# A one-core hybrid decoder step: the GLA and mLSTM branches rewritten as generators that run one step after each weight granule

## The chip, the cores and the metric

The kernel runs on one core of one Trainium2 chip. The core has a matrix engine (PE in the profile, with its weight loads as PEld), a vector engine (DVE), an activation engine (ACT), GpSimd (POOL) and a sequencer that only issues transfers (SP); POOL and ACT can issue transfers too. Each engine takes its instructions in a fixed order. The metric is the device time of one execution in microseconds, the median of the runs shown.

## What is computed

One layer of a recurrent decoder for 256 prompt rows and 8 × 4 sample rows, 288 columns in all, everything in fp32. The heads of the reference are these:

```python
proj = xn @ P['w_in']
(lru_x, g_q, g_k, g_v, g_lr, g_gate, m_x, m_o, m_if, mg) = jnp.split(proj, _split_points(), axis=-1)
...
o, gla_S_new = gla_chunked(q, k, v, logdec.reshape(B, T, GLA_HEADS, GLA_DK), gla_S)
y_gla = rmsnorm(o.astype(dt), P['gla_g_norm']).reshape(B, T, GLA_HEADS * GLA_DV) * jax.nn.silu(g_gate)
...
mq = blockdiag(mc, P['ml_w_q']).reshape(B, T, MLSTM_HEADS, MLSTM_DH)
mk = blockdiag(mc, P['ml_w_k']).reshape(B, T, MLSTM_HEADS, MLSTM_DH) * (MLSTM_DH ** -0.5)
...
h, C_new, n_new, m_new = mlstm_chunked(mq, mk, mv, gates[..., :MLSTM_HEADS], gates[..., MLSTM_HEADS:], ml_C, ml_n, ml_m)
y_ml = jax.nn.sigmoid(m_o) * rmsnorm(h.astype(dt), P['ml_g_norm']).reshape(B, T, MLSTM_WIDTH)
...
merged = (gate[:, :, 0] * (y_lru @ P['w_br_lru'])
          + gate[:, :, 1] * (y_gla @ P['w_br_gla'])
          + gate[:, :, 2] * (y_ml @ P['w_br_ml']))
```

Then come `merged @ w_out`, the residual, a second norm and a squared-ReLU MLP (2048 to 8192 and back) with its residual, and a last norm. Shift, scale and gate of both norms come from `silu(c) @ w_ada`. GLA keeps a state of 128 × 256 for each of 4 heads, mLSTM one of 256 × 257 (memory and normaliser) for each of 4 heads, and the 8 sample sequences bring their own states in and out.

## The kernel before, in words

**The projections.** All weights go through `stream` (lines 148 to 170). A *granule* is a weight tile of 128 × 1024 numbers, 512 KB. SP loads it into one of three `raw` buffers (line 155), ACT rounds it to `hi` (line 156), DVE takes the rest into `lo` (line 157), and PE does 24 matmuls of 288 columns with it (lines 163 to 165): `hi` by the upper and the lower half of the activations, `lo` by the upper half. There are 530 granules and 12,720 such matmuls; this document calls them the main matmuls.

**Work beside them.** `run` (line 184) walks a stream granule by granule. After each it does what `every` lists: `L` loads a tile of `w_ada` (the conditioning weights), `V` multiplies the tiles that are held (line 256). It also takes one step of each generator in `side`; the instructions of such a step are put on every engine behind the granule's last `hi`, `lo` and matmul. `slots` names the buffers that the `w_ada` tiles go to: `None` is a ring of one, a number is one of the ten activation slots, `"st"` the two tiles that also carry the recurrent states.

**The order.** A scheduler that replays a model of the engines sorts the instructions of each engine by readiness and priority. SP's transfers stay in the order of the program. PE, DVE, ACT and POOL wait in order too once the program is built: an instruction whose operand is late holds all behind it.

**The three branches.** The stages are: query, key and value projections; LRU input; gates; `merge(0)` (LRU); `B_MX`; `merge(1)` (GLA); `B_MO`; `merge(2)` (mLSTM); the output projection; the MLP. Each `merge` runs four times a gate block (8 granules) and a branch block (4 granules). LRU is a generator already (line 533). `gla` (line 689) is a plain function that is called once, in `merge(0)`, and `mlstm` (line 900) one that is called after the `B_MX` blocks; all their instructions stand at one place of the program, and the scheduler spreads them as it sees fit.

**GLA.** Cumulative decays, transposed keys and values, the scores, then per head four chunks in sequence through one state buffer `st` (line 770), and a loop over 8 state tiles of the samples: load (line 815), read-out on PE (line 818), update on PE and DVE (lines 825, 826), store (line 827). `spread` (line 679) makes the masked values for it on POOL, 128 × 2048 numbers for each head.

**mLSTM.** A causal convolution (line 530 on DVE), block-diagonal weights (line 915 on POOL), gate rows (lines 930 to 983), values and keys by time (lines 995, 1000), values and keys of the samples (1010, 1017), keys by feature `kf` (line 1022) and queries by feature `qf` (line 1029), then per head the weights `w0`, `w1` (lines 1038 to 1042), scores (1046, 1049), products (1056 to 1062) and the prompt's state (1069). Then a loop over 16 state tiles of the samples: load (line 1109), read-out (1113, 1116), update (1121, 1122), store (1123). All state transfers are issued by POOL, and the state tiles have two buffers (tag `st`). At the end the 8 squares are summed over rows (line 641), the root is inverted on 288 columns (lines 644 to 648) and the outputs are scaled (line 1146).

**The norms.** `rstd_of` (lines 383 to 388) takes the inverse root as Ln and Exp of 128 equal rows of 288.

Of the kernel before, what the change touches and what calls it, by code (L numbers as in the profile page):

```python
# [8 lines left out]
F32 = mybir.dt.float32  # L9
F32R = mybir.dt.float32r  # L10
AF = mybir.ActivationFunctionType
ALU = mybir.AluOpType
# [21 lines left out]
          ("wq", 32), ("wk", 32), ("wv", 32)]  # L34
# [18 lines left out]
def trunk(ctx, tc, io):  # L53
# [328 lines left out]

    def rstd_of(ps):
        r = row("lf")
        with tc.high_priority():
            S.activation(r, ps[:, :N], AF.Ln, bias=eps, scale=1.0 / D)
            S.activation(r, r, AF.Exp, scale=-0.5)
        return r
# [247 lines left out]
    def rows_rsqrt(src, add):  # L636

        p = longp()
        for e in range(2):
            for h in range(4):  # L640
                T.matmul(p[32 * h:32 * h + 32, :N], ones[:, 0:32], src[:, 2 * h + e, :], start=e == 0, stop=e == 1)
        r = row("rr")
        if add is None:
            S.activation(r, p[:, :N], AF.Sqrt, bias=eps, scale=1.0 / 256)
        else:
            V.scalar_tensor_tensor(r, p[:, :N], 1.0 / 256, add, ALU.mult, ALU.add)
            S.activation(r, r, AF.Sqrt)
        V.reciprocal(r, r)
        return r

    def by_sequence(qm, q):

        G.memset(qm, 0.0)
        G.tensor_copy(qm.rearrange("p n (b j) -> p n b j", b=NB)[:, :, :, 0:TS], smp(q))
# [13 lines left out]
    def parts(dst, src, sel, los):  # L668

        w = src.shape[-1]  # L670
        p = misc()
        T.matmul(p[:, 0:w], sel, src, start=True, stop=True)
        S.copy(dst, p[:, 0:w])
        for a, b in los:
            V.tensor_tensor(out=dst[a:b], in0=p[a:b, 0:w], in1=dst[a:b].bitcast(F32), op=ALU.subtract)

    def spread(vx, v, w):

        G.tensor_tensor(out=vx, in0=v.bitcast(F32).unsqueeze(1).to_broadcast([P, NB, w]),
                        in1=C("bcol").unsqueeze(2).to_broadcast([P, NB, w]), op=ALU.mult)  # L680
# [8 lines left out]
    def gla():  # L689
        g_cs, ee, kk_ = slot(4), slot(5), slot(3)  # L690
        wg2 = flat(kk_)[:, 4 * N:4 * N + 512]
        G.memset(wg2, 0.0)
        G.dma_start(wg2[0:32], io["wg2"])
        bg = Pm("bg")
        for h in range(4):
            p = misc()
            T.matmul(p[:, :N], wg2[:, h * P:(h + 1) * P], sm, start=True, stop=True)
            softlog(g_cs[:, h, :], p[:, :N], bg[:, h:h + 1], ee[:, h, :])
        S.activation(ee[:, 0:4], ee[:, 0:4], AF.Exp, scale=-1.0)
        S.activation(ee[:, 0:4], ee[:, 0:4], AF.Ln, bias=1.0)  # L700
        G.tensor_tensor(out=g_cs[:, 0:4], in0=g_cs[:, 0:4], in1=ee[:, 0:4], op=ALU.subtract)
        rm = resets(row("gc"), 0.0, 1.0, 64)
        for h in range(4):
            V.tensor_tensor_scan(g_cs[:, 4 + h, :], rm, g_cs[:, h, :], 0.0, ALU.mult, ALU.add)
        cs = g_cs[:, 4:8, :]
        TAU = 1.0 / 16
        S.activation(ee[:, 0:4], cs, AF.Exp, scale=TAU)
        S.activation(ee[:, 4:8], cs, AF.Exp, scale=-TAU)
# [3 lines left out]
        d_ = g_cs[:, 0:4, :]  # L712
        csp, dp = (a[:, :, 0:NP].rearrange("p h (c l) -> p h c l", c=4) for a in (cs, d_))
        V.tensor_tensor(out=dp, in0=csp[:, :, :, 63:64].to_broadcast([P, 4, 4, 64]), in1=csp, op=ALU.subtract)
        css, ds_ = smp(cs), smp(d_)
        G.tensor_tensor(out=ds_, in0=css[:, :, :, 3:4].to_broadcast([P, 4, NB, TS]), in1=css, op=ALU.subtract)
        S.activation(d_, d_, AF.Exp, scale=TAU)
        qe, ke = qk[:, 0:4, :], qk[:, 4:8, :]
        V.scalar_tensor_tensor(qe, qe, 128 ** -0.5, ee[:, 0:4], ALU.mult, ALU.mult)
        kd = kk_[:, 0:4, :]  # L720
        G.tensor_tensor(out=kd, in0=ke, in1=d_, op=ALU.mult)
# [4 lines left out]
        for t in range(2):  # L726
            for q in range(2):
                p = misc()
                for i in range(4):
                    T.transpose(p[:, i * P:(i + 1) * P], vv[:, 4 * q + i, t * P:(t + 1) * P], ident)  # L730
                S.copy(vt[:, t, 512 * q:512 * q + 512], p)
        vs = sc([P, 257], "vs", 1)
# [9 lines left out]
        S.copy(ks, p[:, 0:P])  # L742

# [5 lines left out]
        for c in range(2):  # L749
            for t in range(2):  # L750
                if c:
                    V.tensor_scalar(kdt[c][:, t, :], pk[t], C("half")[:, c:c + 1], None, ALU.mult)
                else:
                    S.activation(kdt[c][:, t, :], pk[t], AF.Copy, scale=C("half")[:, c:c + 1])

        bb = flat(slot(9))
        am = bb[:, 0:1024].rearrange("p (t h i) -> p t h i", t=2, h=4)
        st = bb[:, 1024:2048].rearrange("p (h e) -> p h e", h=4)
        for t in range(2):
# [5 lines left out]
            V.scalar_tensor_tensor(am[:, t], C("glo").unsqueeze(1).to_broadcast(bc), -1.0, am[:, t], ALU.mult, ALU.min)  # L765
        oT = slot(5)
        for h in range(4):
            po = longp()
            for e in range(2):
                for t in range(2):  # L770
                    c0 = e * 256 + t * P
                    T.matmul(po[:, c0:c0 + P], vt[:, t, h * 256 + e * P:h * 256 + (e + 1) * P], am[:, t, h, :],
                             start=e == 0 and t == 0, stop=False, skip_group_check=True)
            for c in range(4):
                if c:
# [637 lines left out]
```

## Time and profile before

| | |
|---|---|
| median of 3 runs (lowest, highest) | 2022.71 us (2020.01, 2024.82) |
| the profiled execution, its time | 2018.23 us |
| its span on the core | 2016.5 us |
| mean granted PE clock | 0.99 |
| PE busy | 1962.6 us, 97% |
| DVE, ACT, POOL busy | 1027.0, 805.7, 289.3 us |

A row of the groups of instructions reads: line, engine, operation, output and inputs, sizes, count, then busy time and mean duration, then the engine's idle time ahead of it and what ended it. A row of the timeline reads: start, duration, engine, line, operation. One of the stretches has, for each engine, busy time and count, then PE's clock as a share of full speed. A matmul of fp32 operands leaves two records, a main matmul one.

### The profile page before, as it was taken

How to read it: one execution, taken by the hardware profiler on the slowest of the kernel's cores; microseconds unless marked ns; L12 is line 12 of the kernel's file. 1: busy time of each engine (PE TensorE's matmuls, PEld its weight loads, DVE VectorE, ACT ScalarE, POOL GpSimd, SP SyncE). 2: the span in 40 equal slices, each digit the busy share in tenths (PEclk: the TensorE clock that was granted, in tenths of full speed). 3: DMA queues.
4: the chain of work that ended last, by engine and by line, in shares of the span. 5: the costliest groups of instructions: out<-in, count | busy, mean ns of one | idle time of the engine just before them, and what ended most of it. 6: DMA issues, size and time to landing. Idle time of an engine off the chain costs nothing.

```text
span 2016.5 us, 35281 instructions
## 1 busy us (share of the span) xinstructions
PE 1962.6 (97%) x14838; PEld 1838.8 (91%) x14838; DVE 1027.0 (51%) x1436; ACT 805.7 (40%) x1107; POOL 289.3 (14%) x339
## 2 busy tenths in 40 slices
PE   6999999999999999899999999999999999999997
PEld 4889888999997998799999989999999999999997
DVE  3463647646692466543444564335444444444564
ACT  3333464533364332333333454443343434343434
POOL 0300200212231223100011441000010101010101
PEclk8999999999999999899999999999999999999998
DMA  9988756546642377676779736654444454455443
GB/s 372 397 325 308 269 199 237 205 168 240 211 153 73 124 259 253 209 258 250 263 257 356 272 123 224 230 197 159 174 160 157 163 182 158 159 173 171 157 159 119
DMA packets 119438, 429.48 MB, mean 213 GB/s; under 512 B 11744, under 2 KB 11904, under 8 KB 119152
## 3 DMA queue, kind: packets, MB, share of 16 engines
q1 hardware_dynamic: 109776, 392.56, 54.9%
q0 software_dynamic: 7920, 28.92, 4.0%
q10 hardware_dynamic: 1584, 5.75, 0.8%
q8 instruction: 116, 1.90, 0.4%
q14 instruction: 42, 0.34, 0.1%
HBM read 410.38 MB, written 16.81 MB: 212 GB/s over the span
## 4 chain that ended last, share of the span: by engine, by line
PE 87%; DMA 5%; DVE 4%; issue 2%; ACT 1%; POOL 0%; SPq 0%; DVEq 0%; ACTq 0%; POOLq 0%
PE mm L163 26%; PE mm L165 26%; PE mm L164 25%; PE pa L256 4%; DMA raw<-win 3%; DVE lo L157 1%; DMA st<-mC 1%; DVE s L530 1%; DMA s<-wada 1%; ACT hi L156 1%; DMA o_C_s<-st 0%; PE px L579 0%; PE px L1069 0%; PE pi L1113 0%; PE px L781 0%
## 5 line engine op out<-in xcount | busy, mean ns | idle before, releaser
L157 DVE TENSOR_TENSOR lo<-raw,hi 128x1024 fp32r<-128x1024 f32 x450 | 583.7, 1299 | 626.9 <-ACT hi L156 612.0
L156 ACT ACTIVATE hi<-raw 128x1024 fp32r<-128x1024 f32 x450 | 476.4, 1060 | 831.4 <-PE mm L164 618.2
L163 PE MATMUL mm<-xh,hi 128*128 128x288 f32 x2576 | 761.6, 299 | 11.8 <-ACT hi L156 4.7
L164 PE MATMUL mm<-xl,hi 128*128 128x288 f32 x2576 | 759.3, 297 | 0.1
L165 PE MATMUL mm<-xh,lo 128*128 128x288 f32 x2576 | 739.3, 297 | 4.4 <-DVE lo L157 4.4
L163 PEld LDWEIGHTS mm<-xh,hi 128*128 128x128 f32 x2576 | 484.6, 189 | 36.5 <-issue 17.8
L163 PE MATMUL mm<-s,hi 128*128 128x288 f32 x1664 | 489.4, 297 | 0.0
L164 PEld LDWEIGHTS mm<-xl,hi 128*128 128x128 f32 x2576 | 486.2, 189 | 3.4 <-issue 2.1
L164 PE MATMUL mm<-s,hi 128*128 128x288 f32 x1664 | 489.0, 296 | 0.0
L165 PEld LDWEIGHTS mm<-xh,lo 128*128 128x128 f32 x2576 | 478.7, 189 | 8.6 <-DVE lo L157 5.9
L165 PE MATMUL mm<-s,lo 128*128 128x288 f32 x1664 | 476.4, 295 | 0.4 <-DVE lo L157 0.4
L163 PEld LDWEIGHTS mm<-s,hi 128*128 128x128 f32 x1664 | 311.8, 188 | 6.1 <-issue 5.4
L164 PEld LDWEIGHTS mm<-s,hi 128*128 128x128 f32 x1664 | 312.5, 188 | 0.3
L165 PEld LDWEIGHTS mm<-s,lo 128*128 128x128 f32 x1664 | 308.2, 188 | 2.7 <-issue 1.7
L157 DVE TENSOR_TENSOR lo<-s,hi 128x1024 fp32r<-128x1024 f32 x80 | 98.0, 1225 | 115.3 <-ACT hi L156 115.3
L1251 POOL TENSOR_TENSOR t<-t 128x288 f32<-128x288 f32 x64 | 60.5, 954 | 647.6 <-ACT t L1250 647.6
L156 ACT ACTIVATE hi<-s 128x1024 fp32r<-128x1024 f32 x80 | 84.9, 1061 | 143.3 <-PE mm L164 140.0
L881 POOL TENSOR_TENSOR s<-s,t 128x288 f32<-128x288 f32 x32 | 32.2, 1030 | 207.3 <-DVE t L880 207.3
L1267 DVE TENSOR_TENSOR s<-s,mm 128x288 f32<-128x288 f32 x96 | 40.3, 451 | 33.9 <-PE mm L165 32.6
L256 PE MATMUL pa<-s,silc 128*32 128x512 f32 (+1 forms) x480 | 51.7, 526 | 5.5 <-DMA s<-wada 5.5
L425 DVE TENSOR_TENSOR s<-t,s 128x288 fp32r<-128x288 f32 x64 | 33.9, 568 | 16.6 <-ACT s L424 16.6
L1122 DVE SCALAR_TENSOR_TENSOR st<-st,csb,px 128x257 f32<-128x257 f32 x64 | 28.5, 479 | 23.6 <-PE px L1121 15.9
(358 smaller groups left out, 1144.7 us busy)
## 6 DMA issues: line engine op xcount, KB each, us to landing
raw<-win SPq DMA_DIRECT2D x192, 512.0 KB, 4.7
raw<-wf SPq DMA_DIRECT2D x176, 512.0 KB, 4.2
s<-wada SPq DMA_DIRECT2D x47, 1024.0 KB, 8.9
s<-wf SPq DMA_DIRECT2D x80, 512.0 KB, 3.5
ag<-wada SPq DMA_DIRECT2D x29, 1024.0 KB, 6.0
raw<-wout SPq DMA_DIRECT2D x32, 512.0 KB, 6.0
st<-wada SPq DMA_DIRECT2D x28, 512.0 KB, 6.8
s<-win SPq DMA_DIRECT2D x14, 768.0 KB, 6.8
```

What stands on the lines that cost most here:

```text
L156: pace["hi"] = S.activation(hi, raw, AF.Copy)
L157: pace["lo"] = V.tensor_tensor(out=lo, in0=raw, in1=hi.bitcast(F32), op=ALU.subtract)
L163: T.matmul(pss[m][:, :N], hi[:, kk, ms], xh, start=k == k0, stop=False)
L164: T.matmul(pss[m][:, :N], hi[:, kk, ms], xl, start=False, stop=False)
L165: pace["last"] = T.matmul(pss[m][:, :N], lo[:, kk, ms], xh, start=False, stop=k == kt - 1)
L256: pace["prod"] = T.matmul(ps[32 * j:32 * j + 32, h * w // 4:(h + 1) * w // 4], stat(k), v[:, j], start=k == 0 and h == 0, stop=k == KT - 1 ...
L425: V.tensor_tensor(out=dst_l[:, r], in0=src[:, r], in1=dst_h[:, r].bitcast(F32), op=ALU.subtract)
L530: V.scalar_tensor_tensor(y[:, m, s:NP], x[:, m, 0:NP - s], w[:, m, j:j + 1], y[:, m, s:NP], ALU.mult, ALU.add)
L881: G.tensor_tensor(out=a, in0=a, in1=t, op=ALU.add)
L1122: V.scalar_tensor_tensor(s4[:, i, d, :], s4[:, i, d, :], csb[:, h, b:b + 1], pu[:, 0:257], ALU.mult, ALU.add)
L1251: G.tensor_tensor(out=r, in0=r, in1=r, op=ALU.mult)
L1267: V.tensor_tensor(out=a, in0=a, in1=p, op=ALU.add)
```

## The change

`gla`, the gate rows and `mlstm` become generators in `side`, each cut by `yield` into steps of a few instructions, and what they produced as return values goes into lists that `merge` reads when it needs them (`finish`). Inside, the loops over state tiles are written as tables of steps (`do(step, function)`). mLSTM's step table loads a state tile three steps ahead of its use, and slot 9 adds two buffers to the two of `st`. GLA keeps the four chunk states of a head apart (in an `st` tile), so that the products of a chunk no longer stand between two updates of the state.

mLSTM's scores are taken as `mc` by `tf`, where `tf` is `mc` through W_k W_q^T, a block-diagonal product made from the new parameter `wk4`; `kf` is gone, and `qf` is made for the 32 sample columns only. Inverse roots transpose the row blocks, so that ACT's square root and DVE's reciprocal work on 9 columns, and transpose them back. `spread` goes from POOL to ACT, some elementwise operations from POOL to DVE. In the `B_MO` stage the second buffer of the `w_ada` tiles is slot 8 in place of `"st"`.

The core of the diff:

```diff
+    def inv_sqrt(r, src, **ka):
+
+        with tc.high_priority():
+            t = t288()
+            V.transpose(t, src)
+            c = sc([P, N // 32], "rsc", 1)
+            S.activation(c, t[:, 0:N:32], AF.Sqrt, **ka)
+            V.reciprocal(c, c)
+            V.transpose(r.rearrange("p (a b) -> p a b", b=32), c.unsqueeze(2).to_broadcast([P, N // 32, 32]))
+        return r
+
     def rstd_of(ps):
-        r = row("lf")
-        with tc.high_priority():
-            S.activation(r, ps[:, :N], AF.Ln, bias=eps, scale=1.0 / D)
-            S.activation(r, r, AF.Exp, scale=-0.5)
-        return r
+        return inv_sqrt(row("lf"), ps[:, :N], bias=eps, scale=1.0 / D)
...
+    def spread(vx, v, half):
+
+        for b in range(4 * half, 4 * half + 4):
+            S.activation(vx[:, b], v.bitcast(F32), AF.Copy, scale=C("bcol")[:, b:b + 1])
+
+    def steps(at):
+
+        for s in range(max(at) + 1):
+            for f in at.get(s, ()):
+                f()
+            yield
...
-    def spread(vx, v, w):
-
-        G.tensor_tensor(out=vx, in0=v.bitcast(F32).unsqueeze(1).to_broadcast([P, NB, w]),
-                        in1=C("bcol").unsqueeze(2).to_broadcast([P, NB, w]), op=ALU.mult)
...
-                ygla.extend(gla())
+                gla_.append(beside(gla()))
+            if br == 1 and b == 0:
+                finish(gla_[0])
+            if br == 2 and b == 0:
+                finish(ml_)
+                mrg.extend([slot(0, F32R), slot(1, F32R), slot(2, F32R), slot(3, F32R)])
...
-        mc = slot(5)
-        for _ in conv(mx, mc, Pm("mcw"), Pm("mcb"), "mst", "o_mconv", slot(1)):
-            pass
...
+        mc = slot(5)
+        yield from conv(mx, mc, Pm("mcw"), Pm("mcb"), "mst", "o_mconv", slot(1))
...
+        wqk = sc([P, 8, 4], "wqk", 1)
+        w4 = t288()[:, 0:128].rearrange("p (n c d) -> p n c d", n=8, c=4)
+        V.tensor_tensor(out=w4, in0=Pm("wk4").rearrange("p (n c d) -> p n c d", n=8, c=4),
+                        in1=Pm("wq").rearrange("p (n d) -> p n d", n=8).unsqueeze(2).to_broadcast([P, 8, 4, 4]), op=ALU.mult)
+        V.tensor_reduce(out=wqk, in_=w4, axis=AX.X, op=ALU.add)
...
-        kf = slot(2)
         for n in range(8):
             p = misc()
-            T.matmul(p[:, :N], bdk[:, n * P:(n + 1) * P], mc[:, n, :], start=True, stop=True)
-            S.copy(kf[:, n, :], p[:, :N])
...
+            T.matmul(p[:, :N], bdv[:, n * P:(n + 1) * P], mc[:, n, :], start=True, stop=True)
+            S.copy(tf[:, n, :], p[:, :N])
+            if n % 2:
+                yield
+
+        qs = e0[:, 2048:2304].rearrange("p (n i) -> p n i", n=8)
+        p = misc()
         for n in range(8):
...
+            T.matmul(p[:, n * NS:n * NS + NS], bdq[:, n * P:(n + 1) * P], mc[:, n, NP:N], start=True, stop=True)
...
-                T.matmul(p[:, 0:256], kf[:, n, 0:P], qf[:, n, 0:NP], start=e == 0, stop=e == 1)
+                T.matmul(p[:, 0:256], mc[:, n, 0:P], tf[:, n, 0:NP], start=e == 0, stop=e == 1)
...
+        def ends():
+            p = misc()[:, 0:64].rearrange("p (h d b) -> p h d b", h=4, d=2)
+            for h in range(4):
+                for d in range(2):
+                    T.matmul(p[:, h, d], kp[:, h, d * P:(d + 1) * P], vn, start=True, stop=True)
+            V.tensor_copy(pnb, p)
+
+        def load(n):
+            i = n % 4
+            tiles[n] = sp.tile([P, 1028], F32, tag="st", name=nm("st"), bufs=2) if i < 2 else s9[:, 1028 * (i - 2):1028 * (i - 1)]
+            G.dma_start(tiles[n], io["mC"][n])
...
+        def when(n):
+            return 5 + n * 3 // 2
...
+        for n in range(16):
+            do(when(n), tile_, n)
+            do(when(n) - 3, load, n)
...
-    nT = mlstm()
+    mos = []
+    ml_ = beside(mlstm())
 
     merge(1, ygla, io["wbg"])
-    slots.update(ids=(None, "st"), n=0)
+    slots.update(ids=(None, 8), n=0)
     every("L L . V . . .", skip=5)
...
-                S.activation(sc([P, 1], "warm", 1), ssum[:, 0:1], AF.Ln)
+                S.activation(sc([P, 1], "warm", 1), ssum[:, 0:1], AF.Sqrt)
```

Three places of the built order. **SP, in the first `B_MO` block**: `raw` is a granule's buffer, `ag` the ring, `st` a state tile, `s` a slot. Before:

```order
L155 DMA raw_8171<-win 128x1024
L295 DMA ag_8201<-wada 128x2x1024
L155 DMA raw_8203<-win 128x1024
L293 DMA st_8233<-wada 128x1024
L293 DMA st_8234<-wada 128x1024
L155 DMA raw_8237<-win 128x1024
L155 DMA raw_8275<-win 128x1024
```

Now, in the change:

```order
L155 DMA raw_8071<-win 128x1024
L295 DMA ag_8101<-wada 128x2x1024
L155 DMA raw_8116<-win 128x1024
L295 DMA s_1115_8146<-wada 128x2x1024
L155 DMA raw_8178<-win 128x1024
L155 DMA raw_8234<-win 128x1024
```

The place in SP's queue is the same; the buffer that the load waits for is slot 8 in place of two state tiles, and the weights behind it are the same ones.

**POOL, in the loop over mLSTM's state tiles**: `o_C_s` is the output in memory, `mC` the input. Before:

```order
L1123 DMA o_C_s<-st_6225 128x1028
L1109 DMA st_6278<-mC 128x1028
L1123 DMA o_C_s<-st_6258 128x1028
L1109 DMA st_6297<-mC 128x1028
L1123 DMA o_C_s<-st_6278 128x1028
L1109 DMA st_6316<-mC 128x1028
```

Now:

```order
L1276 DMA o_C_s<-st_7156 128x1028
L1246 DMA st_7421<-mC 128x1028
L1276 DMA o_C_s<-st_7192 128x1028
L1246 DMA st_7472<-mC 128x1028
L1276 DMA o_C_s<-s_951_7017 128x1028
L1246 DMA s_951_7017<-mC 128x1028
```

Store and load alternate as before, and each load still takes the buffer of the store just ahead of it; but the load is of the tile four on (before: two on), and every second pair of tiles lies in slot 9.

**PE, at mLSTM's heads** (`px` are short-lived banks, `mm` those of the main matmuls). Before, the heads follow one another:

```order
L127 MATMUL px_5860<-row_5659,con 128x256
L1046 MATMUL px_5870<-s_808_5833,s_797_5797 128x256 x2
L1049 MATMUL px_5870<-s_808_5833,s_797_5797 128x128 x2
L1056 MATMUL px_5877<-t_820_5862,s_784_5720 128x256
L1056 MATMUL px_5877<-t_821_5863,s_784_5720 128x128
```

Now one step of a head stands between two granules:

```order
L164 MATMUL mm_6549<-s_709_5289,hi_6675 128x288
L165 MATMUL mm_6549<-s_708_5288,lo_6676 128x288
L1207 MATMUL px_6716<-s_785_5916,s_801_6014 128x256
L1207 MATMUL px_6716<-s_785_5916,s_801_6014 128x128
L1207 MATMUL px_6716<-s_785_5916,s_801_6014 128x256
L1207 MATMUL px_6716<-s_785_5916,s_801_6014 128x128
L1212 MATMUL px_6722<-s_785_5916,ones 128x256
L1213 MATMUL px_6722<-s_785_5916,ones 128x128
L163 MATMUL mm_6727<-xh_106,hi_6732 128x288
```

Before, 54 rows in a run (82 matmuls, from the samples' values at line 1010 to the scores of the fourth head) hold no main matmul; now about 24 of them stand between one step and the next. The main matmuls keep their own order.

More of the change, by code (lines that the diff above doesn't have):

```diff
@@ L634, in softlog @@
         V.tensor_scalar(dst, p, bias, 0.0, ALU.add, ALU.min)
[L636 to L649, printed above, removed]
     def by_sequence(qm, q):
         G.memset(qm, 0.0)
-        G.tensor_copy(qm.rearrange("p n (b j) -> p n b j", b=NB)[:, :, :, 0:TS], smp(q))
+        G.tensor_copy(qm.rearrange("p n (b j) -> p n b j", b=NB)[:, :, :, 0:TS], q)
     def quarters(t):
@@ L1151, in trunk @@
+        yield from steps(at)
+        while not mos:
+            yield
+        mo = mos[0]
+        y = slot(8, F32R), slot(9, F32R)
+        for h in range(4):
+            a = slice(2 * h, 2 * h + 2)
+            V.scalar_tensor_tensor(nT[:, a], mo[:, a], 1.0, nT[:, a], ALU.add, ALU.mult)
+            scaled_rows(y, nT, sums, h)
+            yield
+        yml.extend(y)
+    mos = []
+    ml_ = beside(mlstm())
     merge(1, ygla, io["wbg"])
-    slots.update(ids=(None, "st"), n=0)
+    slots.update(ids=(None, 8), n=0)
```

551 lines of the change are left out of this document (338 added, 213 removed), and 1 row of the table PARAMS.

## Prediction

> **What bounds the kernel now.** I read the page first, for who is busy.
>
> ```profile
> span 2016.5 us, 35281 instructions
> PE 1962.6 (97%) x14838; PEld 1838.8 (91%) x14838; DVE 1027.0 (51%) x1436; ACT 805.7 (40%) x1107; POOL 289.3 (14%) x339
> ```
>
> PE is the bound, and only 54 us of the span are without it. No rearrangement can gain more than PE's gaps, the time PE runs below full clock, and PE work that goes away. So the second view is the busy time by stretch, cut at the stages of the change (PE busy, PEld, DVE, ACT, POOL, PE clock, DMA share, GB/s):
>
> ```profile
> 340.00:575.00 235.00, 233.20 (x1773) 214.64 (x1773) 142.53 (x176) 95.08 (x129) 50.59 (x53) 1.00 0.57 196
> 575.00:600.00 25.00, 23.08 (x171) 22.64 (x170) 25.00 (x40) 19.24 (x27) 9.88 (x16) 1.00 0.45 137
> 600.00:625.00 25.00, 25.00 (x201) 25.00 (x200) 11.28 (x23) 12.41 (x24) 0.95 (x3) 1.00 0.50 164
> 625.00:672.00 47.00, 43.08 (x245) 33.15 (x244) 11.17 (x26) 17.55 (x42) 13.15 (x24) 1.00 0.10 35
> 672.00:835.00 163.00, 159.08 (x1241) 148.38 (x1240) 93.37 (x142) 50.16 (x64) 44.41 (x48) 1.00 0.70 227
> 835.00:855.00 20.00, 13.15 (x65) 10.14 (x65) 11.91 (x20) 11.39 (x16) 0.53 (x1) 0.74 0.67 226
> 855.00:1200.00 345.00, 344.51 (x2675) 318.19 (x2674) 167.15 (x228) 135.23 (x191) 63.50 (x77) 1.00 0.70 256
> 1200.00:2000.00 800.00, 800.00 (x6030) 794.40 (x6029) 389.43 (x496) 319.41 (x412) 69.40 (x74) 1.00 0.50 172
> ```
>
> The last row is the clean state: 6030 matmuls in 800 us, 132.7 ns each, so a granule of 24 takes 3.18 us. The gaps lie in four places, all inside the branches that the change rewrites: the convolution with DVE full (575 to 600), mLSTM's heads (625 to 672), its state loop (672 to 835) and the end of that loop (835 to 855).
>
> The last is the largest for its length. SP's own waits and timeline tell why:
>
> ```profile
> SPq L293 <- DMA o_C_s<-st: 25.7, 2, 20.7
> 813.98 0.33 SPq L155 DMA_DIRECT2D raw<-win  x1
> 835.31 5.80 SPq L293 DMA_DIRECT2D st<-wada  x2
> 841.20 11.27 SPq L155 DMA_DIRECT2D raw<-win  x6
> 845.99 1.06 ACT L156 ACTIVATE hi<-raw 128x1024 fp32r<-128x1024 f32 x1 [5.70 <-DMA raw<-win]
> ```
>
> After 814 SP stands 20.7 us at a conditioning load that wants a state tile, until the tile's last store has landed. The weights queued behind it leave at 841.20, and ACT rounds the next one at 845.99: PE has run dry.
>
> **The change part by part**, against the profiled execution of 2018.23 us.
>
> *SP's wait (835 to 855).* PE is idle 20.00 − 13.15 = 6.85 us. Part of what it does there runs slowly:
>
> ```profile
> 840.00:845.00 5.00, 2.26 (x4) 1.18 (x4) 2.89 (x3) 0.29 (x1) 0.00 (x0) 0.73 0.64 215
> 845.00:850.00 5.00, 2.90 (x11) 2.76 (x11) 2.44 (x4) 2.31 (x3) 0.00 (x0) 0.50 0.66 235
> 850.00:855.00 5.00, 5.00 (x28) 4.75 (x27) 3.90 (x7) 4.62 (x7) 0.00 (x0) 0.75 0.78 242
> 842.42 2.26 PE L127 MATMUL px<-row,con 128*128 128x288 f32 x4 [3.28 <-DVE row L648]
> ```
>
> The clock lost is 0.27 × 2.26 + 0.50 × 2.90 + 0.25 × 5.00 = 3.3 us. [...] In the change the load goes to slot 8. Its last readers are the matmuls of `merge(1)`'s branch block, and in the built order eight granules' weights (178 to 185) stand between the end of that stage and the load, so nothing waits. The row of 842.42 is the second half of the stall: PE also stood behind the reciprocal of 288 columns; now the rows are inverted two steps before their use and `merge(1)` and `B_MO` granules run in between. Gain **10.1** (0 if SP finds another wait).
>
> *mLSTM's heads (625 to 672).* 47.00 − 43.08 = 3.92 us idle, since 82 matmuls follow one another and each waits for the weights `w0`, `w1` or a bank. With a granule (3.18 us) between two steps the cover is there. Gain **3.9**.
>
> *The convolution (575 to 600).* DVE is busy all 25 us, `lo` comes late, PE is idle 1.92 us. One feature tile per granule instead: **1.9**.
>
> *The state loop (672 to 835).* 3.92 us idle, each time at a tile that had not landed. Who waits there:
>
> ```profile
> POOL st L1109 <- DMA o_C_s<-st: 62.3, 13, 6.8
> POOL o_C_s L1123 <- DVE st L1122: 34.6, 11, 11.7
> st<-mC POOLq DMA_DIRECT2D x16, 514.0 KB, 4.4
> o_C_s<-st POOLq DMA_DIRECT2D x16, 514.0 KB, 5.7
> L1123 POOL DMA_DIRECT2D o_C_s<-st x16: 531/533/580, 707.4 to 836.3; - x16
> ```
>
> A tile takes (836.3 − 707.4) / 15 = 8.6 us: with two buffers, POOL issues a store, waits for it to land (5.7 from issue), issues the load (0.53), then waits for the update of the tile just loaded. With four buffers the last wait goes, and POOL's turn is 5.7 + 0.53 = 6.2 us at least. PE's turn is one and a half granules, 4.8 us, and some 1.8 us of its own products: 6.6. POOL is as fast, barely. A load leaves three steps ahead of use, some 13 us, and needs 0.5 + 4.4. Gain **3.9**, and the rival below is this margin.
>
> *GLA (340 to 575).* 1.8 us idle; half lies at its start, where the chain stays as long: **1.0** (0 to 1.8).
>
> *PE's own work.* `kf` goes: 8 matmuls as `qf`'s in this row; the added small ones are like the second row:
>
> ```profile
> 628.07 4.96 PE L1022 MATMUL px<-s,s 128*128 128x288 f32 x16 [0.49 <-ACT vs L1011]
> L127 PE MATMUL px<-srow,con 128*128 128x32 f32 x8 | 1.2, 257 | 0.0
> ```
>
> Minus 4.96. `qs` is 8 matmuls of 32 columns; the row has 4 of them in 1.2 us, so at most 2.4, at least half as they follow one another; the 8 of 8 columns in `ends` are no dearer than 0.5. Net gain **3.2** (2.1 to 4.0).
>
> *The roots.* At the very end nothing covers them:
>
> ```profile
> 2001.32 2.42 PE L381 MATMUL pi<-t,ones 128*128 128x288 f32 x8 [0.24 <-ACT t L375]
> 2002.81 1.28 ACT L386 ACT_TABLE_LOAD   x1
> 2004.62 1.28 ACT L387 ACT_TABLE_LOAD   x1
> 2006.39 1.73 DVE L1295 TENSOR_TENSOR s<-s,row 128x576 f32<-128x576 f32 x2 [4.34 <-ACT row L387]
> L219 DVE STREAM_TRANSPOSE t<-pa 128x256 f32<-128x256 f32 x13 | 5.2, 432 | 20.6 <-PE pa L256 20.6
> 1175.84 0.23 ACT L1237 ACTIVATE xh<-row 128x32 fp32r<-128x32 f32 x1
> ```
>
> From PE's last record (2003.74) to DVE's first scaling are 2.65 us. Now: a transpose, 432 × 288 / 256 = 486 ns; a root of 9 columns, no more than the 0.23 of 32; a reciprocal, put as long; a transpose back; four hand-overs of 0.1: 1.8. In the built order no table load stands in the MLP or at the end, since the square root's was loaded ahead of it. Gain **0.9** (−0.5 to 1.3). In the middle norm PE is idle at most 0.49 (the row 855 to 1200): left out.
>
> *What is added.* `spread` on ACT is 64 instructions, priced by the nearest row of 256 columns:
>
> ```profile
> L1003 ACT ACTIVATE s<-px,acol 128x256 f32<-128x256 f32 x8 | 3.4, 470 | 2.0 <-PE px L1000 2.0
> L679 POOL TENSOR_TENSOR s<-s,con 128x2064 fp32r<-128x2064 f32 x4 | 14.6, 3638 | 7.0 <-DVE s L675 5.9 <-PE px L1121 1.1
> ```
>
> That is 30 us on ACT over some 300 us where it is busy 40%, for 29 us off POOL; queued behind are the `hi` of later granules, and behind those PE. In the built order DVE's and ACT's operations of a step come with two or three later granules already rounded, a cover of 6 us. About 120 steps now stand between granules; each is a place where PE can wait in order. The nearest row is GLA's, whose instructions were interleaved already: 1.8 us idle in 235. Over the some 500 us that the steps cover that is **−4** (0 to −12).
>
> Sum: 10.1 + 3.9 + 1.9 + 3.9 + 1.0 + 3.2 + 0.9 − 4 = 20.9. The profiled execution would take 2018.2 − 20.9 = 1997.3. It lies 4.5 below the median of 2022.71; with the same distance the median is about **2002**.
>
> **The rivals.**
>
> *SP's wait only moves.* The load of slot 8, the ring or the later state tiles of `merge(2)` could hold the weights as `"st"` did. For: SP is one queue. Against: the readers named above are done. Then the 10.1 stay lost: 2012.
>
> *POOL's queue paces the state loop.* If a POOL turn stays at 8.6 us in place of 6.6, 12 loads fall 24 us behind; the cover of some 13 us goes first, and PE waits the remaining 11: 2013. It decides from a turn of about 7.6 us on. For: the store must land before the next store may even be issued, and 4 accumulations wait there too. Against: POOL's other wait, 34.6 us over 11, has lost its cause. [...]
>
> *Slower: the steps block the rounding.* Each step's ACT and DVE instructions wait for PE's step, and `hi` and `lo` queue behind. If the real lag is longer than the scheduler's model, PE pays at each step. It decides at (20.9 + 4) / 120 = 0.21 us a step; at 0.4 us it costs 48 and the time is 2026. For: the model was wrong by more than that at 814. Against: the two granules of cover, and GLA's row.
>
> The change cannot fail to do what it says: the buffers and the order are built in.
>
> **How the numbers follow.** The forecast, with a gain of 15 to 31, has 0.75; SP's wait elsewhere 0.08; POOL's pace 0.10; the steps 0.07. The range takes the forecast's unknowns (stalls 0 to 12, the bounds of GLA, PE work and root, the clock) and reaches to the first two rivals: 1991 to 2013. A difference below 0.2% (4 us) can't be told from none here. Faster by more: the first case and most of the next two, 0.88. Within: 0.06. Slower: 0.06.
>
> **What would show it.** Right: SP's waits hold no entry above 5 us for `wada` behind `o_C_s`; no stretch between 340 and 860 has PE below 97%, and the clock stays at 1.00 there; POOL's stores come every 6.5 us or so; between PE's last record and the first scaling are under 2 us. The forecast is wrong if PE's idle time between 340 and 860 stays above 10 us, or if the stretch from 1200 to 2000 changes.

## The result and the profile after

| | before | after |
|---|---|---|
| median of the runs on the same chip | 2021.36 us (2019.85 to 2024.82, 4 runs) | 1999.62 us (1996.96 to 2000.26, 4 runs) |
| ratio, with its 95% interval | | 0.9888 (0.9870 to 0.9905) |
| the profiled execution, its time and span | 2018.23, 2016.5 us | 1999.18, 1997.4 us |
| PE busy; span less PE busy | 1962.6; 53.9 us | 1960.1; 37.3 us |

The change is faster by 1.1%. The forecast was 2002 with a range of 1991 to 2013; its sum of 20.9 us stands against 19.1 between the two spans: 16.6 less idle time and 2.5 less busy time. The page of the changed kernel begins so:

```profile
span 1997.4 us, 35369 instructions
PE 1960.1 (98%) x14830; PEld 1839.4 (92%) x14830; DVE 1018.1 (51%) x1496; ACT 820.3 (41%) x1153; POOL 250.2 (13%) x330
```

Busy time by stretch, cut at the places of the change (PE busy, PEld, DVE, ACT, POOL, PE clock, DMA share, GB/s):

```profile
340.00:530.00 190.00, 190.00 (x1433) 170.73 (x1431) 100.25 (x148) 84.13 (x126) 14.11 (x28) 1.00 0.59 209
530.00:600.00 70.00, 70.00 (x515) 68.47 (x514) 52.72 (x85) 40.46 (x54) 17.05 (x24) 1.00 0.49 160
600.00:672.00 72.00, 72.00 (x566) 69.91 (x565) 28.70 (x40) 31.59 (x55) 19.98 (x33) 1.00 0.37 125
672.00:795.00 123.00, 122.81 (x903) 114.04 (x902) 69.53 (x132) 51.81 (x87) 21.12 (x31) 1.00 0.62 196
795.00:800.00 5.00, 1.58 (x10) 0.76 (x11) 1.13 (x5) 0.82 (x1) 0.00 (x0) 0.72 1.01 403
800.00:805.00 5.00, 5.00 (x21) 3.79 (x20) 1.19 (x2) 0.00 (x0) 3.55 (x6) 0.60 0.91 335
1180.00:1980.00 800.00, 800.00 (x6030) 794.40 (x6029) 390.07 (x495) 320.43 (x414) 70.64 (x75) 1.00 0.49 172
```

The MLP stage is as it was, 6030 matmuls in 800 us. GLA, the convolution and the heads are without a gap. One stall is new, at 795: 3.42 us idle in that row, and 0.28 × 1.58 + 0.40 × 5.00 = 2.4 us of clock lost in it and the next, 5.9 us in all. First the timeline of SP, then that of POOL, then PE's at that place:

```profile
789.08 1.28 SPq L295 DMA_DIRECT2D ag<-wada  x1
794.44 0.61 SPq L295 DMA_DIRECT2D s<-wada  x1
```

```profile
772.23 0.54 POOL L1276 DMA_DIRECT2D o_C_s<-st  x1
779.94 0.53 POOL L1246 DMA_DIRECT2D st<-mC  x1 [7.17 <-DMA o_C_s<-st]
780.47 0.54 POOL L1276 DMA_DIRECT2D o_C_s<-st  x1
789.41 0.53 POOL L1246 DMA_DIRECT2D st<-mC  x1 [8.40 <-DMA o_C_s<-st]
```

```profile
794.52 0.29 PE L165 MATMUL mm<-xh,lo 128*128 128x288 f32 x1
798.42 1.09 PE L1262 MATMUL pi<-st,s 128*32 128x257 f32 x8 [3.61 <-DMA st<-mC]
```

State tile 9 uses the buffer of tile 5. Its load leaves only when the store of 780.47 has landed, at 789.41, and lands at 798.4, as PE starts on it. That store was late itself: POOL first stood 7.17 us for the store of 772.23 to land, to issue the load ahead of it. SP no longer waits for a state tile's store; its conditioning loads now leave at 789.08 and 794.44, beside this load. So two suspects stand next to each other, POOL's wait for the store and the crowd of loads. The landing times rose (median from issue to landing, in the list of transfers; before they were 4.4 and 5.7):

```profile
st<-mC POOLq DMA_DIRECT2D x8, 514.0 KB, 6.3
o_C_s<-st POOLq DMA_DIRECT2D x8, 514.0 KB, 7.0
```

At the end, DVE and ACT behind PE's last record (1985.44):

```profile
1985.55 0.48 DVE L387 STREAM_TRANSPOSE t<-pi 128x288 f32<-128x288 f32 x1 [1.81 <-PE pi L381]
1986.07 0.31 ACT L389 ACTIVATE rsc<-t,eps 128x9 f32<-128x9 f32 x1 [1.58 <-DVE t L387]
1986.41 0.21 DVE L390 RECIPROCAL rsc<-rsc 128x9 f32<-128x9 f32 x1 [0.38 <-ACT rsc L389]
1986.66 0.48 DVE L391 STREAM_TRANSPOSE row<-rsc 128x288 f32<-128x288 f32 x1
1987.17 1.73 DVE L1490 TENSOR_TENSOR s<-s,row 128x576 f32<-128x576 f32 x2
```

From 1985.44 to the first scaling are 1.73 us, where it was 2.65. The four operations take 1.48 of them; the hand-overs between the rows, put at 0.1 each in the prediction, take 0.03 to 0.04, and the first, from PE to DVE, 0.11.

### The profile page after: what moved, and what is told of

The parts are those of the page before. It is cut to its first block, busy times and chain, and to the rows that moved or that the text cites. A ratio compares the mean times of both kernels' runs of the same rounds, so it can differ in the third digit from the quotient of the medians.

```text
span 1997.4 us, 35369 instructions
## 1 busy us (share of the span) xinstructions
PE 1960.1 (98%) x14830; PEld 1839.4 (92%) x14830; DVE 1018.1 (51%) x1496; ACT 820.3 (41%) x1153; POOL 250.2 (13%) x330
## 4 chain that ended last, share of the span: by engine, by line
PE 93%; DMA 4%; DVE 2%; issue 0%; ACT 0%; POOL 0%; DVEq 0%; ACTq 0%; SPq 0%; POOLq 0%
PE mm L163 28%; PE mm L165 27%; PE mm L164 27%; PE pa L256 5%; DMA s<-wada 1%; DMA o_C_s<-st 1%; DVE s L537 1%; DMA s<-x 1%; DVE lo L157 0%; DMA st<-mC 0%; PE px L586 0%; PE px L817 0%; DMA o_C_s<-s 0%; PE px L1197 0%; PE pi L1262 0%
## 5 line engine op out<-in xcount | busy, mean ns | idle before, releaser
L157 DVE TENSOR_TENSOR lo<-raw,hi 128x1024 fp32r<-128x1024 f32 x450 | 558.2, 1242 | 611.8 <-ACT hi L156 583.2
L256 PE MATMUL pa<-s,silc 128*32 128x512 f32 (+1 forms) x496 | 54.3, 523 | 6.0 <-DMA s<-wada 6.0
L256 PEld LDWEIGHTS pa<-s,silc 128*32 128x32 f32 x496 | 14.6, 112 | 27.1 <-issue 14.5
```

Source lines behind the costliest of these rows:

```text
L157: pace["lo"] = V.tensor_tensor(out=lo, in0=raw, in1=hi.bitcast(F32), op=ALU.subtract)
L256: pace["prod"] = T.matmul(ps[32 * j:32 * j + 32, h * w // 4:(h + 1) * w // 4], stat(k), v[:, j], start=k == 0 and h == 0, stop=k == KT - 1 ...
```

## The experiments

Each ratio is to the kernel before on the same chip; the changed kernel's is 0.9888, and 0.001 is 2 us.

### The slot alone, in the kernel before

```diff
-    slots.update(ids=(None, "st"), n=0)
+    slots.update(ids=(None, 8), n=0)
```

> The kernel before with one edit: in the B_MO stage the second buffer of the conditioning tiles is slot 8 in place of the state tiles. Theory 1 (the wait is worth its row): SP no longer stands 20.7 us behind a state tile's store, and the 6.85 us of idle PE and 3.3 us of lost clock at 835 to 855 come back: 2021 - 10 = 2011 us, with nothing new in their place. Theory 2 (the loads collide): the conditioning tiles now leave some 20 us earlier, into the state loop's own transfers, a state tile lands late there, and PE loses about what it lost in the changed kernel (3.4 us idle and 2.4 of clock): a gain of 4 only, 2017 us. A third outcome, no gain at all (2020 to 2022), would mean that SP's queue only waits at the next place.

Median 2012.99 us, ratio 0.9953 (0.9939 to 0.9967). The stall at 835 is gone in its profile (first row; 13.15 busy before), but PE waits longer for state tiles (second row; 3.8 us in 7 before):

```profile
835.00:855.00 20.00, 19.66 (x150) 16.29 (x149) 9.78 (x14) 7.78 (x12) 1.07 (x2) 1.00 0.59 202
```

```profile
PE pi L1113 <- DMA st<-mC: 8.3, 5, 3.0
```

The spans differ by only 1.7 us. The same kernel was run again:

> The kernel before with slot 8 in place of the state tiles in B_MO, once more, since the first execution profiled lay 3.6 us above its own median and the profile of before 3 to 6 below its, so that the two profiles differ by 1.7 us and the medians by 9.5. Theory 1 (the wait is worth its row, the loop's waits are scatter): ratio 0.994 to 0.997 again, the stall at 835 to 855 gone in the profile, idle time of PE behind mC loads (line 1113) anywhere between 4 and 8 us. Theory 2 (the loads collide in the loop): the wait of line 1113 is 8 us or more again, and the median gains 5 or less.

Ratio 0.9967 (0.9953 to 0.9981), and the profile has the loop's wait again, larger:

```profile
PE pi L1113 <- DMA st<-mC: 9.7, 6, 3.5
```

This profile is 2.6 us longer than that of before. By the ratios the slot is worth 9.5 and 6.7 us. In both profiles the stall at 835 is gone, and the loop lost most of that: from 672 to 835 PE is idle for 7.93 and 9.43 us where it was 3.92, at a clock of 0.98 and 0.97 where it was 1.00. Some 1.6 us of clock went far ahead of it, from 575 to 600 (0.93 in both, 1.00 before). The wait was worth its row, as theory 1 has it. That the loop waits more is not the collision of theory 2, since nearly all of these waits come before the first conditioning load of the stage leaves. In the first of the two profiles, the last long wait and that load:

```profile
797.12 1.08 PE L1113 MATMUL pi<-st,s 128*32 128x257 f32 x8 [2.73 <-DMA st<-mC]
```

```profile
819.25 0.43 SPq L295 DMA_DIRECT2D ag<-wada  x1
```

Behind it PE waits for a state tile 0.34 us more, and in the second profile, where the load leaves at 822.90, 0.27. What else slows the loop stays open, and how much it takes can't be read from single executions, since this loop scatters: the runs of this kernel lie between 2011.32 and 2020.91, those of before, over all the chips used, between 2017.36 and 2028.36.

### The steps taken out

```diff
-                gla_.append(beside(gla()))
+                for _ in gla():
+                    pass
+                gla_.append(None)
...
-    gt_ = beside(gates())
+    gt_ = gates()
...
-    ml_ = beside(mlstm())
+    ml_ = mlstm()
+    while not ready:
+        next(ml_)
+    beside(ml_)
```

> The changed kernel, but the instructions of GLA, of the gate rows and of mLSTM up to its last root are put into the program at one place each (GLA ahead of the branch block of merge(0), mLSTM ahead of merge(1)), as in the kernel before, and the scheduler spreads them; buffers, slot, scores and roots stay as changed. Theory 1 (the steps fill PE's gaps): the idle time at the convolution (1.9), the heads (3.9), GLA (1.3) and the state loop (3.9) comes back, 7 to 11 us: 2007 to 2011. Theory 2 (the buffers and the slot did it): 1998 to 2002. Theory 3 (the steps themselves cost what the sum has as 4 us of stalls): 1994 to 1997.

Median 2074.20 us, ratio 1.0251 (1.0237 to 1.0265): 51 us slower than before, and none of the theories had that. The state loop, for one, now runs bunched:

```profile
680.00:720.00 40.00, 28.00 (x139) 17.30 (x138) 19.42 (x54) 14.07 (x34) 9.19 (x17) 0.72 0.56 176
720.00:760.00 40.00, 28.48 (x142) 14.67 (x142) 22.99 (x75) 8.25 (x19) 9.62 (x18) 0.67 0.79 246
```

In 40 us PE does 142 matmuls where it did 300 in full stretches, idle for 11.5 and at two thirds of its clock otherwise. So without the steps the new code is worse than the old: the buffers and the slot don't carry the gain by themselves, and with the steps PE has granules to work on between the tiles. The run does not price the steps one by one, since the old code, too, was written for one place and lost far less there. The edit also takes away the high priority that the steps have in the scheduler, and no run parts the two.

### No conditioning loads in the loop's way

```diff
-    every("L L . V . . .", skip=5)
+    every("")
```

> The changed kernel without conditioning loads in the B_MO stage; the four tiles are loaded later, in the stages behind. In the changed kernel PE stood 3.4 us at 795 to 800 for a state tile whose load took 10 us to land, and the clock took 2.4 us more. Theory 1 (contention): the 2 MB of conditioning tiles that left at 789 and 794 slowed that load; without them the tile lands in 6.4 us or less, the stall goes, and the time falls by 4 to 6: 1994 to 1996. Theory 2 (POOL's queue): the load left late, since POOL stood 8.4 us for a store to land that had left at 780, before any conditioning load; the stall stays or shrinks by 1 us: 1998 to 2000.

Median 2007.11 us, ratio 0.9918 (0.9905 to 0.9932). PE's waits:

```profile
PE pi L1262 <- DMA st<-mC: 3.7, 2, 2.7
PE pi L1262 <- DMA s<-mC: 0.9, 1, 0.9
```

The waits for state tiles stay, 4.6 us in 3, with no conditioning tile in flight, so POOL's wait for the stores makes tiles late by itself, as theory 2 has it. Theory 1 still has a part. These are the load of tile 9, PE's start on it, and PE's start on tile 13:

```profile
788.38 0.53 POOL L1246 DMA_DIRECT2D st<-mC  x1 [6.83 <-DMA o_C_s<-st]
```

```profile
795.07 0.64 PE L1262 MATMUL pi<-st,s 128*32 128x257 f32 x8 [1.05 <-DMA st<-mC]
825.20 0.64 PE L1262 MATMUL pi<-st,s 128*32 128x257 f32 x8 [2.65 <-DMA st<-mC]
```

The load of tile 9 lands in 6.7 us in place of 9.0, and its stall is 1.05 us in place of 3.61. PE then runs on and waits at tiles 11 and 13 instead. The four conditioning tiles put off come due at the second norm, where nothing covers them: the output projection takes 5.5 us more (124.19 for 118.66 from its first main matmul to the next stage's) and the MLP 5.4. So the loads were well placed.

### More steps for a tile

```diff
-            return 5 + n * 3 // 2
+            return 5 + n * 7 // 4
```

> The changed kernel with mLSTM's state tiles at every 7/4 steps in place of every 3/2, so a load leaves 4 steps behind the store of its buffer in place of 3, and the loop ends 4 granules later. Theory 1 (the loop's own traffic and POOL's wait for the store): POOL no longer waits for a store, every load is ahead of its use, the stall at 795 goes and the time falls by 4 to 6: 1994 to 1996. Theory 2 (the burst of conditioning loads alone): the tile in flight at 789 to 799 is late again: 1998 to 2000, with a stall of 2 to 4 us at that place. Too slow a loop would show as PE idle at the end of the gate block of merge(2), where the rest of mLSTM is run out.

Median 1999.40 us, ratio 0.9884 (0.9869 to 0.9899). No wait for a state tile is left among PE's, and from 340 to 860 the clock is 1.00, as theory 1 has it, and yet nothing is gained. POOL still waits for stores, against theory 1: tile 9's load leaves at 788.36, hardly earlier than in the changed kernel, and it is PE that comes later, at 801.76. The timeline of PE shows what took its place, the conditioning products (L256) and a head's gather (L704) by turns:

```profile
823.25 1.04 PE L256 MATMUL pa<-ag,silc 128*32 128x512 f32 x2
824.23 0.41 PE L704 MATMUL px<-con,os 128*128 128x32 f32 x2
```

One product of 512 columns, two records, takes 1.04 us here. With seven steps for a head and a pattern of seven for the conditioning tiles the two meet again at the next head, at 857. Next, the same with the conditioning loads two granules earlier:

```diff
-    every("L L . V . . .", skip=5)
+    every("L L . V . . .", skip=3)
```

> The run with tiles at every 7/4 steps, and the conditioning loads of B_MO two granules earlier (the pattern skips 3 granules in place of 5). With 7/4 alone the stall at 795 was gone (idle PE between the gates and the end of merge(2) 0.6 us in place of 4.1, clock 1.00), but the total stayed: PE's conditioning products (L256) took 36.5 us in place of 32.7, since at 823 and 857 the two products of a head's gather (L704) stood between them, and one of them then took 430 to 520 ns in place of about 100. Theory 1 (the interleaving ate the gain): in this order no L704 stands among the L256 of B_MO; L256 falls back to 32.7 or less, the stall stays away, and the time is 4 to 5 us below the changed kernel: a ratio of 0.986 to 0.987. Theory 2 (the loop has its own price wherever it ends): no gain, 0.988 to 0.989.

Median 1993.93 us (1993.23 to 1995.48), ratio 0.9863 (0.9843 to 0.9882), as theory 1 has it. It is faster than the kernel before. Its interval overlaps that of the changed kernel, but its stages from `B_MX` to `merge(2)` take 512.2 us in the profile where the changed kernel's take 516.6. PE's timeline and the groups, of this kernel:

```profile
846.49 1.07 PE L256 MATMUL pa<-ag,silc 128*32 128x512 f32 x8
```

```profile
L256 PE MATMUL pa<-ag,silc 128*32 128x512 f32 (+1 forms) x256 | 33.5, 576 | 0.6 <-DMA ag<-wada 0.6
```

And the group of the run ahead:

```profile
L256 PE MATMUL pa<-ag,silc 128*32 128x512 f32 (+1 forms) x256 | 37.6, 576 | 1.0 <-DMA ag<-wada 1.0
```

Four products in a row, eight records, take what one took between gathers: four of 128 × 32 in 1.07 us against one in 1.04 beside products of 128 × 128. That is 4.1 us of PE for this group. No run shows why.

To part the pace from the place of the loads, the changed kernel with the second edit alone:

> The changed kernel with the conditioning loads of B_MO two granules earlier, state tiles at every 3/2 steps as in the change. Theory 1 (the pace of the loop makes the stall: loads 3 steps behind the store of their buffer): a stall of 2 to 5 us at an mC tile is there again, and the ratio is 0.988 to 0.989, as of the changed kernel. Theory 2 (what helped the best run was the place of the conditioning loads alone): no stall, ratio 0.986 to 0.987.

Median 1997.09 us, ratio 0.9876 (0.9861 to 0.9891), with the stall at the same tile:

```profile
790.00:795.00 5.00, 3.87 (x31) 2.86 (x29) 3.61 (x8) 1.49 (x3) 0.00 (x0) 1.00 1.01 368
795.00:800.00 5.00, 3.21 (x25) 2.42 (x26) 1.49 (x3) 0.79 (x1) 0.02 (x1) 1.00 1.02 391
```

The stall decides for theory 1, that the pace makes it; the ratio lies between the ranges of the two theories. This time the stall did not cost the clock, and the span is 4.0 us shorter than the changed kernel's.

### Two state buffers

```diff
-            tiles[n] = sp.tile([P, 1028], F32, tag="st", name=nm("st"), bufs=2) if i < 2 else s9[:, 1028 * (i - 2):1028 * (i - 1)]
+            tiles[n] = sp.tile([P, 1028], F32, tag="st", name=nm("st"), bufs=2)
```

> The changed kernel with two state buffers in mLSTM's loop in place of four (all 16 tiles from the two of st, each loaded in the step of its predecessor's store, 3 steps ahead as before). Theory 1 (the prediction's: two buffers make the loop wait): store to landing 5.7 to 7, load to landing 4.4 to 6.4, use 1.5, issue 1: 13 to 16 us for a tile where three steps and their products give 13; PE waits up to 3 us at each of 14 tiles, with lost clock behind each: 2015 to 2040. Theory 2 (three steps cover two buffers as well, and the steps alone filled the loop's gaps): 1999 to 2004.

Median 2012.16 us (2004.94 to 2015.51), ratio 0.9944 (0.9924 to 0.9964). PE's waits for state tiles:

```profile
PE pi L1262 <- DMA st<-mC: 9.7, 5, 5.8
```

This is theory 1 in kind, at less than the least it had: five tiles are late, and 0.0056 of the time, 11 us, is what the two other buffers are worth. Steps alone do not fill this loop.

### Scores by keys and queries

```diff
+        kf = slot(0)
         for n in range(8):
+            p = misc()
+            T.matmul(p[:, :N], bdk[:, n * P:(n + 1) * P], mc[:, n, :], start=True, stop=True)
+            S.copy(kf[:, n, :], p[:, :N])
...
-                T.matmul(p[:, 0:256], mc[:, n, 0:P], tf[:, n, 0:NP], start=e == 0, stop=e == 1)
+                T.matmul(p[:, 0:256], kf[:, n, 0:P], tf[:, n, 0:NP], start=e == 0, stop=e == 1)
```

> The changed kernel with mLSTM's scores as before: queries and keys by feature, 8 more products of 288 columns and 8 copies on ACT, in the same four steps; the 8 products of 32 columns for the sample queries go. Theory 1 (the prediction's term): PE does 4.96 more and up to 2.4 less, the time rises by 3.2 (2.1 to 4.0) and merge(1) lengthens by that. Theory 2 (the two traces: PE's work in the middle fell by only 1.6 beside idle time and clock): it rises by about 1.5 to 2.

Median 2000.75 us, ratio 0.9893 (0.9874 to 0.9911), not to be told from the changed kernel. The stage lengths can tell: `merge(1)` takes 209.64 us from its first main matmul to the next stage's, for 207.65. That is 2.0 more, as theory 2 has it. What came back, and (second) what went, in the changed kernel:

```profile
L1142 PE MATMUL px<-s,s 128*128 128x288 f32 x16 | 5.2, 405 | 0.0
```

```profile
L1151 PE MATMUL px<-s,s 128*128 128x32 f32 x16 | 1.9, 271 | 0.0
```

### The norms by Ln and Exp

```diff
-        return inv_sqrt(row("lf"), ps[:, :N], bias=eps, scale=1.0 / D)
+        r = row("lf")
+        with tc.high_priority():
+            S.activation(r, ps[:, :N], AF.Ln, bias=eps, scale=1.0 / D)
+            S.activation(r, r, AF.Exp, scale=-0.5)
+        return r
```

> The changed kernel with the three norms over the model dimension taken as before, by Ln and Exp of 288 columns, and the table of Ln loaded ahead. Theory 1 (the prediction's term): from PE's last record to the first scaling 2.65 us in place of 1.73, the time rises by 0.9. Theory 2 (the table loads stand on the path): both loads of 1.28 appear behind PE's last record, and the rise is 1.5 or more. Theory 3: the middle norm, where PE runs on, changes as well, and the MLP stage lengthens by over 0.3.

Median 2000.84 us, ratio 0.9894 (0.9877 to 0.9912). ACT and DVE at the end, PE's last record being at 1986.71:

```profile
1985.77 1.28 ACT L397 ACT_TABLE_LOAD   x1
1987.06 0.50 ACT L397 ACTIVATE row<-pi,eps 128x288 f32<-128x288 f32 x1
1987.58 1.28 ACT L398 ACT_TABLE_LOAD   x1
1988.88 0.44 ACT L398 ACTIVATE row<-row 128x288 f32<-128x288 f32 x1
1989.35 1.73 DVE L1494 TENSOR_TENSOR s<-s,row 128x576 f32<-128x576 f32 x2 [4.34 <-ACT row L398]
```

From PE's last record to the first scaling are 2.64 us, for 1.73 in the changed kernel; the 0.9 between them is theory 1's. The second table load is the largest part of the path, 1.28 us; the new form has none there. The MLP stage is the same to 0.1 us.

### The masked values on POOL

```diff
-        for b in range(4 * half, 4 * half + 4):
-            S.activation(vx[:, b], v.bitcast(F32), AF.Copy, scale=C("bcol")[:, b:b + 1])
+        a = slice(4 * half, 4 * half + 4)
+        G.tensor_tensor(out=vx[:, a], in0=v.bitcast(F32).unsqueeze(1).to_broadcast([P, 4, 256]),
+                        in1=C("bcol")[:, a].unsqueeze(2).to_broadcast([P, 4, 256]), op=ALU.mult)
```

> The changed kernel with the masked values for the state loops made on POOL as before (16 operations of 128x1024 and some 1.8 us each, in the same steps) in place of 64 operations of 128x256 on ACT. Theory 1 (POOL's queue is the loop's tight one): each stands among the loads and stores, loads leave up to 1.8 us later, and the stalls at mC tiles grow by 3 to 8 us: ratio 0.990 to 0.993. Theory 2 (POOL has room, and ACT's 27 us lay beside other work): the same as the changed kernel, 0.988 to 0.989. Theory 3 (ACT's 27 us delayed the rounding): faster by over 2, 0.987 or less.

Median 1994.94 us, ratio 0.9865 (0.9851 to 0.9878), against 0.9888 (0.9870 to 0.9905) for the change. It looks faster, though the intervals still overlap, and POOL pays more than expected:

```profile
L675 POOL TENSOR_TENSOR s<-s,con 128x1024 fp32r<-128x1024 f32 x16 | 35.5, 2243 | 14.1 <-PE px L883 7.7 <-DVE s L668 6.4
```

Theory 1 falls. The profile has no wait for a state tile, and `B_MO` is 5.7 us shorter (72.08 for 77.74), while `merge(1)` is 1.9 longer (209.54 for 207.65). Two explanations remained, the stall or ACT's 27 us, so both edits that helped were put together:

> Both edits that were faster than the change: state tiles at every 7/4 steps with the conditioning loads two granules earlier, and the masked values on POOL. Each alone gave 0.986 to 0.987. Theory 1 (both gained the same thing, the one stall of 5.9 us at a late state tile with its clock): together they give no more, 0.985 to 0.987, and PE's idle time between the gates and the end of merge(2) stays at about 2 us. Theory 2 (the 27 us on ACT had a price of their own, through late roundings): the two add up, 0.983 to 0.984.

Median 1995.94 us, ratio 0.9866 (0.9839 to 0.9893). This is no more than either alone, as theory 1 has it: both gained the same thing, the one stall with its clock. Why the stall goes with the values on POOL shows in POOL's timeline of the run with that edit alone:

```profile
767.60 0.54 POOL L1277 DMA_DIRECT2D o_C_s<-st  x1 [3.52 <-DVE st L1274]
771.29 0.54 POOL L1247 DMA_DIRECT2D s<-mC  x1 [3.15 <-DMA o_C_s<-s]
783.37 0.53 POOL L1247 DMA_DIRECT2D st<-mC  x1 [6.82 <-DMA o_C_s<-st]
```

POOL's order is another one. The store of tile 4 (767.60) now stands ahead of the load of tile 7 (771.29), so POOL waits for two stores at a time, and tile 9's load leaves at 783.37, 6.0 us earlier than in the changed kernel and before the first conditioning load of the stage (791.99). No run has this order without the rest of the edit, so it is argued from the trace.

## Why the prediction was right, point by point

| term | predicted | measured |
|---|---|---|
| SP's wait | 10.1 | 9.5 and 6.7 alone, by the ratios |
| heads | 3.9 | 3.9 (72.00 of 72.00 busy) |
| convolution | 1.9 | 1.9 |
| state loop | 3.9 | 3.9 gone, see below |
| GLA | 1.0 | 1.8 (no gap left) |
| PE's work | 3.2 | 2.0 (scores put back), 1.6 by the pages |
| end root | 0.9 | 0.9 |
| added stalls | −4 | −5.9, at one place |

*SP's wait.* Right: in the two profiles of the slot alone PE is busy for 19.66 and 19.73 us of the 20, and in the changed kernel SP's list has no wait for a state tile's store. What the term left out is that loads let go earlier meet other transfers: in the changed kernel they made tile 9's load land in 9.0 us, and without them it took 6.7.

*The state loop* is the step that failed in its reasoning. The prediction had a load leave three steps, some 13 us, ahead of its use, and counted 4.9 us for it. In the trace the load of tile 9 left 5.4 us ahead of where PE wanted it (789.41 and 794.8), since the step table only sets its place in POOL's order, and there it waits for the landing of the buffer's store: 8.9 us for that store and 9.0 for the load, where the kernel before had medians of 5.7 and 4.4. This is the rival on POOL's pace, on a small scale. It was to decide from a turn of 7.6 us. Over the whole loop the stores make turns of 6.95 (743.22 to 847.47), but the five turns from 748.02 to 789.94 take 8.4 each. Against the 6.6 that the prediction had for PE's turn they use up 9 of the 13 us of lead, and the long landing of tile 9 did the rest. More steps for a tile took the stall away; taking away the conditioning loads made it smaller at this tile and moved the rest of it to later ones.

*Buffers and scatter.* That the loop was worth more than its 3.9 us was hidden in the base. The runs with two state buffers spread over 5 to 11 us on a chip (of before, 12 runs from 2017.36 to 2025.82; of the experiment, 6 from 2004.94 to 2015.51), the four of each kernel with four buffers over 2 to 6; part of that is that there were fewer of them. The profile of before was a good execution, 4.5 us under the median of three runs that the prediction had (3.1 under that of four), and that of after lies 0.4 under. The assumption that the same distance would hold failed, to the change's favour: about 22 us by medians against 19 by spans. It is argued from these ranges, not shown by a run of its own.

*The added stalls.* The size was near and the cause was not, so that the sizes agree is luck: the one stall is the state loop's, and apart from it PE has no gap in the branches. The steps do have a price, but as busy time. The conditioning products of `merge(0)`, in the kernel before and in the changed one (PE busy, PEld, clock, DMA share, GB/s), and a place in the changed one:

```profile
309.60:517.90 208.30, 11.96 (x96) 2.30 (x96) 0.99 0.59 212
```

```profile
310.90:520.90 210.00, 14.08 (x96) 2.69 (x96) 1.00 0.62 220
```

```profile
415.71 1.05 PE L256 MATMUL pa<-ag,silc 128*32 128x512 f32 x4
416.69 0.70 PE L817 MATMUL px<-s,s 128*128 128x256 f32 x2
```

GLA's products now stand between them, and the same 96 take 2.1 us more. That is a part of why `merge(0)` is 1.7 us longer than before (209.98 for 208.27) although its gaps are filled. No term of the prediction had this.

*PE's work* was mis-sized. `kf` was priced at 4.96 us and the term at 3.2. With `kf` put back and the sample queries (1.9) taken out the stage is 2.0 longer, so `kf` costs some 3.9 there. The 8 products of `ends`, put at no more than 0.5, take 0.9 (line 1240). By the pages PE's work fell by 1.6 (2.5 less busy time, of which 3.3 − 2.4 = 0.9 is clock), after the 2.1 above.

*The clock.* The stall of 3.4 us cost 2.4 us of it, that of before 3.3 in 6.85, and one of 2.9 us in the run with the earlier loads nothing (1.00 in both its rows). In the run without conditioning loads a stall of 2.65 us, shorter than that one, left a clock of 0.66 from 825 to 830, where PE is busy for 4.80 us: 0.34 × 4.80 = 1.6 us. So the length of a stall alone does not decide what it costs, and what does is not shown. The prediction counts the clock among the unknowns of its range, and no run shows a bound for it; what the runs show is a loss of 0 to 3.3 us at a stall.

*The slower rival* (steps blocking the rounding) did not come: behind 340 PE waits nowhere for `hi`, and 0.4 us for `lo`. Its price in the prediction is a wrong sum: 0.4 us at 120 steps is 48 us, and with the other 24.9 us gained that gives about 2046, not 2026; 2026 belongs to some 0.23 us a step. Of the signs that the prediction named, two were not met in full: PE between 340 and 860 (busy above 97% with the clock at 1.00 throughout), at 795 to 805, and POOL's stores, which come every 6.95 us on average but every 8.4 ahead of the stall.

## What to carry to other kernels

Read a load's lead from what its queue waits for, not from where the program puts it: with a ring of buffers it is the store's landing that releases the load (here tile 9's, 8.9 us after the store left), and landings lengthened as the loop was made faster (a store from 5.7 to 7.0 us). A mean over the loop hides this; look at the turns just ahead of a stall. A stretch that is filled this well (122.81 of 123.00 us busy ahead of the stall) turned here on one collision, 3.42 us idle and 2.4 of clock; two periodic tasks on one engine with the same period meet every time or never, and shifting one by two steps was worth about 4 us here by the ratios. And look at the scatter of the runs: a loop that waits for transfers may show it in the range (here 5 to 11 us with two buffers, 2 to 6 with four) before it shows in one profile.

## What the runs showed that was not expected

Products of 128 × 32 take longer where products of 128 × 128 stand between them: one of 512 columns in 1.04 us, against four in a row in 1.07. The changed kernel itself pays this in `merge(0)`, where 96 records take 14.08 us for 11.96. With weights, state and conditioning loads in flight together (DMA share 0.9 to 1.0) a transfer of 514 KB took up to 10.9 us in the changed kernel (the store issued at 789.94), against a median of 5.7 and at most 7.0 before.
